# The last MLP of a decoder layer: its up product as seven products of quarter matrices

## The chip, the cores and the metric

The kernel runs on one core of a Trainium2 chip. What counts is the device time of one execution in microseconds (us). Before the change the median of three runs is 1575.95 us (1574.12 to 1577.76). The engines are PE (matrix products; its weight loads are listed apart as PEld), DVE (vector), ACT (scalar and activation), POOL (GpSimd, elementwise work from SBUF only) and SP (it issues most DMA transfers, in order).

## What is computed

One layer of a decoder on 1024 prompt tokens and 32 sample tokens, model width 1024: modulated norm, one input projection, stick-breaking attention in eight heads and a gated recurrence in eight heads, an output projection, and a squared-ReLU MLP. For this change only the MLP matters:

```python
h2 = rms_norm(x, n2) * (1 + sc2) + sh2
x = x + g2 * (jnp.square(jax.nn.relu(h2 @ w_up)) @ w_down)   # w_up (1024, 4096), w_down (4096, 1024)
```

All of it is float32. The kernel writes each factor of a product as a sum of two rounded parts, `hi` and `lo`, and adds three matmuls: hi by hi, hi by lo, lo by hi. Making the two parts (`split`, L147 to L150) is a cast on ACT and a subtraction on DVE or POOL.

## The kernel before

The program is one long list of instructions for each engine, laid down by a scheduler from generators that the source interleaves. In order of time: input projection and recurrence; the first attention; the output projection of prompt tokens 0 to 511; then the first MLP (those 512 tokens) interleaved with the decode of the sample tokens and the second attention (tokens 512 to 1023); the second output projection (`out_projection`, token tiles in the order 4, 5, 8, 6, 7, where 8 is the 32 sample tokens); the last MLP on tokens 512 to 1055, 544 columns in all.

`mlp` (L1171) serves both MLPs. It goes through eight blocks of 512 hidden units. In a block the up product takes four weight pieces of 1024 by 128 (`piece`, loaded in one transfer each into the ring `wraw` of the pool `weights`, split into `whi` and `wlo`), and for each it makes 128 hidden units by all columns: eight contraction steps of three matmuls (L202 to L204). Each result is evicted by ACT (relu L1189, cast L1191) and DVE (square L1190, subtraction L1192) into `uh` and `ul`, which are the moving factors of the down product. The down product adds 8 x 128 output columns into the accumulators `acc` (DVE, L1250). In the last MLP the 544 columns go as a chunk of 256 and one of 288, and weights stand still while columns move. The ring `wraw` has existed since the start of the program, so the scheduler may issue a weight load long before its use.

`modulate` (L307) makes the columns of the last MLP's input from the normalised rows of a tile: transposes on PE (`ptx`, L314), scale and shift on ACT (`hf`, L319) or DVE, the cast `h_hi` (L328) on DVE and the subtraction `h_lo` (L329) on DVE or POOL. The rows of a tile are scaled at L1161 (`xr`), after the sums of squares and a reciprocal root of eleven tiny DVE operations (L134 to L142).

Two generators are interleaved in the middle of the program by weights, the first MLP (`WM` = 64 for its steps) and decode with the second attention (`W[3]` = 166):

```python
x = min(steps, key=lambda x: (x[2] + 0.5) / x[1])   # the one that is least far along goes next
```

The output projection's first weights (`woraw`, L1111), the reads of x (`xres`, L1231) and the stores of the first MLP's results (`out_dram`, L1237) stand in SP's queue in a fixed order and go one after another.

Of the kernel before, what the change touches and what calls it, by code (L numbers as in the profile page):

```python
# [20 lines left out]
P = 128  # L21
D = 1024
# [22 lines left out]
CS = ((256,),(256,))  # L45
# [16 lines left out]
NFX = 8  # L62
# [17 lines left out]
def hymba_step(ctx, tc, x_p, x_s, ck, cv, st_in, ptab, c_p, c_s, w_ada, b_ada, n1g, n2g, w_in,  # L80
# [226 lines left out]
    def modulate(pl, xn, r, c0, a, b, hi_all, lo_all, bufs, kind="r", nu=NU, e=None, ks=(range(4), range(4, 8)), hs=None):  # L307

        for kr in ks:
# [18 lines left out]
            V.tensor_copy(hi_all[:, kk, c0:c0 + r], hf)  # L328
            (e or (G if g and r == P else V)).tensor_tensor(lo_all[:, kk, c0:c0 + r], hf, hi_all[:, kk, c0:c0 + r].bitcast(F32), op=sub)  # L329
# [690 lines left out]
    HW = 544  # L1020
    mmbank = lambda shape, name: bank("mm", shape, name)
# [29 lines left out]
    def out_projection(pl, wpl, tiles, t0, h_hi, h_lo, ks, parts):  # L1051
# [77 lines left out]
        for i, t in enumerate(tiles):  # L1129
# [16 lines left out]
            with tc.high_priority(offset=PN if t in (3, 7) else PN0):  # L1146
# [15 lines left out]
                modulate(pl, xx, r, t * P - t0, a2, b2, h_hi, h_lo, 2)  # L1162
# [6 lines left out]
    def mlp(h_hi, h_lo, t0, chunks, fp, nx, side=iter(())):  # L1169
# [4 lines left out]
        res = {}  # L1174
        if n > 512:
            res_s = fp.tile([NS, D], F32, name="res_s")
            nc.sync.dma_start(res_s, x1d[T:TA, :])
        else:
            g2b = fp.tile([P, D], F32, name="g2b")
        acc = [lp.tile([P, HW], F32, name=f"acc{c}", tag="acc", bufs=8) for c in range(KT)]  # L1180
        for blk in range(NBLK):
            u_hi, u_lo, ws = [], [], []
            cuts = (0,) + CS[t0 > 0] + (n,)
# [24 lines left out]
            if n == 512 and blk == NBLK - 1:  # L1208
                nc.sync.dma_start(g2b, g2d.to_broadcast([P, D]))
            for half_ in range(2) if n == 512 else ():  # L1210
# [29 lines left out]
            for c in range(KT) if n > 512 else ():  # L1240
# [3 lines left out]
                if blk < NBLK - 1:  # L1244
                    def out_y(ci, pm):
                        cs = chunks[ci]
# [4 lines left out]
                    stationary_weights(*w, u_hi, u_lo, NK, chunks, mlpbank, out_y)  # L1251
                else:

                    cc = slice(c * P, (c + 1) * P)
                    g2s = g2[:, c, 1:9].unsqueeze(2).to_broadcast([P, NB, 4])
                    samp = lambda a: a.rearrange("p (b t) -> p b t", t=4)
                    S.activation(acc[c][:, 0:512], acc[c][:, 0:512], AF.Identity, scale=g2[:, c, 0:1])
                    if n > 512:
                        V.tensor_tensor(samp(acc[c][:, 512:n]), samp(acc[c][:, 512:n]), g2s, op=mult)
                    for cs in chunks[::-1]:  # L1260
                        def out_y(_, pm):
                            e = min(cs.stop, 512) - cs.start
                            V.scalar_tensor_tensor(acc[c][:, cs.start:cs.start + e], pm[:, 0:e], g2[:, c, 0:1],
                                                   acc[c][:, cs.start:cs.start + e], op0=mult, op1=add)
                            if cs.stop > 512:
                                ys = fp.tile([P, NS], F32, name="ys", bufs=2)
                                V.tensor_tensor(samp(ys), samp(pm[:, e:e + NS]), g2s, op=mult)
                                V.tensor_tensor(acc[c][:, 512:n], acc[c][:, 512:n], ys, op=add)
                        stationary_weights(*w, u_hi, u_lo, NK, [cs], mlpbank, out_y)
                        with tc.high_priority(offset=PY):  # L1270
                            o, nt = cs.start, (min(cs.stop, 512) - cs.start) // P
                            rows = slice(t0 + o, t0 + o + nt * P)
                            view = lambda a, c0, w: a[rows, P * c0:P * (c0 + w)].rearrange("(u p) c -> p u c", p=P)
                            if c % 2 == 0:
                                res[o] = fp.tile([P, nt, 2 * P], F32, name="xres", tag="xres", bufs=nx)
                                nc.sync.dma_start(res[o], view(x1d, c, 2))
                            xr = res[o][:, :, P * (c % 2):P * (c % 2 + 1)]
                            pt = bank("y", [P, 4, P], "pty")
                            for u in range(nt):
                                TE.transpose(pt[:, u, :], acc[c][:, o + u * P:o + (u + 1) * P], ident)  # L1280
                            if cs.stop > 512:
                                TE.transpose(pt[:NS, nt, :], acc[c][:, 512:n], ident)
                            V.tensor_tensor(xr, pt[:, :nt], xr, op=add)
                            if c >= KT - YS:
                                nc.sync.dma_start(view(y_p, c, 1), xr)
                            elif c % 2 == 1:
                                nc.sync.dma_start(view(y_p, c - 1, 2), res[o])
# [45 lines left out]
    for _ in mlp(*h2, 512, [slice(0, 256), slice(256, 544)], pool("final"), NFX):  # L1333
        pass
# [32 lines left out]
```

## Time and profile before

| | |
|---|---|
| median of 3 runs | 1575.95 us |
| profiled execution | 1573.13 us |
| its span, first to last instruction | 1571.4 us |
| PE busy | 1522.4 us (97%) |
| DVE busy | 980.1 us (62%) |
| ACT busy | 623.9 us (40%) |
| POOL busy | 356.2 us (23%) |
| mean DMA rate | 142 GB/s |
| mean granted TensorE clock | 0.988 of full speed |
| chain of waits that ended last, by engine | PE 81%, DVE 8%, DMA 6% |

Busy shares are means over stages with different limits; a stage is read by the wait that ends last in it. Matmuls are pipelined, so the spacing of their starts, and not the duration of one, is what a matmul costs PE.

### The profile page before, as it was taken

How to read it: one execution, taken by the hardware profiler on the slowest of the kernel's cores; microseconds unless marked ns; L12 is line 12 of the kernel's file. 1: busy time of each engine (PE TensorE's matmuls, PEld its weight loads, DVE VectorE, ACT ScalarE, POOL GpSimd, SP SyncE). 2: the span in 40 equal slices, each digit the busy share in tenths (PEclk: the TensorE clock that was granted, in tenths of full speed). 3: DMA queues.
4: the chain of work that ended last, by engine and by line, in shares of the span. 5: the costliest groups of instructions: out<-in, count | busy, mean ns of one | idle time of the engine just before them, and what ended most of it. 6: DMA issues, size and time to landing. Idle time of an engine off the chain costs nothing.

```text
span 1571.4 us, 26224 instructions
## 1 busy us (share of the span) xinstructions
PE 1522.4 (97%) x9629; PEld 1276.1 (81%) x9629; DVE 980.1 (62%) x2084; ACT 623.9 (40%) x1187; POOL 356.2 (23%) x568
## 2 busy tenths in 40 slices
PE   7999999999999989999998999999899999999998
PEld 3666689998998777765566788888479999999998
DVE  4976438888866862444544977887585344444445
ACT  3742244444423453432232665655345322233330
POOL 0200125544210120000111776793110000000000
PEclk8999999999999989999998999999999999999999
DMA  9389873533124466667465374642744222322221
GB/s 327 110 282 308 259 216 67 111 65 76 50 62 143 135 193 216 204 220 248 150 153 126 98 139 99 137 117 90 234 149 146 87 89 87 94 82 86 89 82 58
DMA packets 249413, 223.14 MB, mean 142 GB/s; under 512 B 60507, under 2 KB 196259, under 8 KB 247236
## 3 DMA queue, kind: packets, MB, share of 16 engines
q1 hardware_dynamic: 186308, 199.26, 40.4%
q0 software_dynamic: 62976, 22.20, 8.4%
q8 instruction: 76, 1.25, 0.3%
q14 instruction: 53, 0.43, 0.1%
HBM read 190.14 MB, written 31.11 MB: 141 GB/s over the span
## 4 chain that ended last, share of the span: by engine, by line
PE 81%; DVE 8%; DMA 6%; issue 2%; ACT 2%; POOL 1%; SPq 0%; POOLq 0%; ACTq 0%; DVEq 0%
PE pm L202 15%; PE pm L203 15%; PE pm L204 15%; PE pm_qkv L215 3%; PE pm L1219 3%; PE pm_qkv L213 3%; PE pm_qkv L214 3%; PE pm L1221 3%; PE pm L1220 3%; PE pod L675 2%; PE ptd L625 2%; DMA wraw<-in_w_up_dram 1%; PE ptw L922 1%; DVE om L909 1%; PE pm_o L1143 1%
## 5 line engine op out<-in xcount | busy, mean ns | idle before, releaser
L202 PE MATMUL pm<-h_hi,whi 128*128 128x288 f32 (+3 forms) x1184 | 384.3, 326 | 4.9 <-DVE gg L792 1.7
L203 PE MATMUL pm<-h_lo,whi 128*128 128x288 f32 (+3 forms) x1184 | 381.9, 323 | 0.3 <-DVE h_lo L329 0.2
L204 PE MATMUL pm<-h_hi,wlo 128*128 128x288 f32 (+3 forms) x1184 | 380.9, 322 | 0.0
L149 ACT CAST whi<-wraw 128x1024 fp32r<-128x1024 f32 x160 | 167.9, 1052 | 317.9 <-PE pm L203 211.5
L150 DVE TENSOR_TENSOR wlo<-wraw,whi 128x1024 fp32r<-128x1024 f32 x144 | 185.1, 1286 | 157.5 <-ACT whi L149 151.6
L202 PEld LDWEIGHTS pm<-h_hi,whi 128*128 128x128 f32 x1184 | 223.6, 189 | 27.0 <-issue 9.8
L204 PEld LDWEIGHTS pm<-h_hi,wlo 128*128 128x128 f32 x1184 | 224.0, 189 | 10.3 <-issue 1.2
L203 PEld LDWEIGHTS pm<-h_lo,whi 128*128 128x128 f32 x1184 | 223.8, 189 | 9.6 <-DVE h_lo L329 0.9
L203 PE MATMUL pm<-ul,whi 128*128 128x256 f32 (+1 forms) x512 | 145.7, 288 | 0.0
L204 PE MATMUL pm<-uh,wlo 128*128 128x256 f32 (+1 forms) x512 | 145.5, 288 | 0.0
L202 PE MATMUL pm<-uh,whi 128*128 128x256 f32 (+1 forms) x512 | 143.7, 289 | 0.0
L909 DVE TENSOR_TENSOR_SCAN om<-om 128x128 f32<-128x128 f32 (+3 forms) x96 | 110.1, 1151 | 27.1 <-POOL om L903 18.8
L150 POOL TENSOR_TENSOR wlo<-wraw,whi 128x1024 fp32r<-128x1024 f32 x16 | 38.5, 2406 | 389.6 <-ACT whi L149 344.1
L910 POOL TENSOR_TENSOR be<-be,om 128x384 f32<-128x384 f32 (+3 forms) x96 | 100.2, 1053 | 51.5 <-DVE om L909 45.2
L1219 PE MATMUL pm<-whi,uh 128*128 128x512 f32 x256 | 106.1, 415 | 2.4 <-DVE acc L1227 2.2
L1221 PE MATMUL pm<-whi,ul 128*128 128x512 f32 x256 | 103.1, 406 | 1.6 <-DVE ul L1192 1.6
L1220 PE MATMUL pm<-wlo,uh 128*128 128x512 f32 x256 | 102.4, 401 | 0.0
L204 PEld LDWEIGHTS pm<-uh,wlo 128*128 128x128 f32 x512 | 95.9, 188 | 0.0
L203 PEld LDWEIGHTS pm<-ul,whi 128*128 128x128 f32 x512 | 95.9, 188 | 0.0
L202 PEld LDWEIGHTS pm<-uh,whi 128*128 128x128 f32 x512 | 94.6, 188 | 0.1
L1250 DVE TENSOR_TENSOR acc<-acc,pm 128x256 f32<-128x256 f32 (+1 forms) x96 | 41.0, 436 | 69.2 <-PE pm L204 69.2
L215 PE MATMUL pm_qkv<-whi,h_lo 128*128 128x512 f32 x192 | 77.6, 405 | 0.8 <-DVE h_lo L329 0.8
(354 smaller groups left out, 2860.9 us busy)
## 6 DMA issues: line engine op xcount, KB each, us to landing
wraw<-in_w_up_dram SPq DMA_DIRECT2D x64, 512.0 KB, 4.0
wraw<-in_w_down_dram SPq DMA_DIRECT2D x64, 512.0 KB, 4.8
wada<-in_w_ada_dram SPq DMA_DIRECT2D x16, 1024.0 KB, 9.1
raw<-in_cache_k_dram SPq DMA_DIRECT2D x64, 256.0 KB, 3.3
vt<-in_cache_v_dram SPq DMA_DIRECT2D x64, 256.0 KB, 3.9
wraw<-in_w_in_dram SPq DMA_DIRECT2D x24, 512.0 KB, 5.7
wa<-in_w_ada_dram SPq DMA_DIRECT2D x16, 512.0 KB, 6.4
qkd<-th SPq DMA_DIRECT2D x16, 256.0 KB, 7.1
```

Source lines behind the costliest of these rows:

```text
L149: (V.tensor_copy if h is V else S.copy)(hi, src)
L150: (e or V).tensor_tensor(lo, src, hi.bitcast(F32), op=sub)
L202: TE.matmul(pm, w_hi[:, k, :], r_hi[k][:, cs], start=(k == 0), stop=False)
L203: TE.matmul(pm, w_hi[:, k, :], r_lo[k][:, cs], start=False, stop=False)
L204: TE.matmul(pm, w_lo[:, k, :], r_hi[k][:, cs], start=False, stop=(k == nk - 1))
L213: TE.matmul(pm, h_hi[:, k, cs], hi, start=(k == 0), stop=False)
L215: TE.matmul(pm, h_lo[:, k, cs], hi, start=False, stop=(k == KT - 1))
L909: V.tensor_tensor_scan(back, back, back, 1.0 if right is None else right[:, 0:1], op0=mult, op1=ALU.bypass)
L910: G.tensor_tensor(be[:, 0:w], be[:, 0:w], om[:, 1:w + 1], op=mult)
L1219: TE.matmul(pm, u_hi[m][:, ts], hi, start=(m == 0), stop=False)
L1220: TE.matmul(pm, u_hi[m][:, ts], lo, start=False, stop=False)
L1221: TE.matmul(pm, u_lo[m][:, ts], hi, start=False, stop=(m == NK - 1))
```

## The change

The last MLP leaves `mlp` and gets a function of its own, `last_mlp`. `mlp` keeps the first 512 tokens only; its last `yield` moves out of the down loop, so that the first MLP has one more step in each block (70 steps in all, where there were 62).

The 544 columns become two halves of 272: tiles 4 and 5 with 16 sample tokens, tiles 6 and 7 with the other 16. Two neighbouring blocks of 128 hidden units form a *unit*; its weights are a 2 x 2 array of quarters (two column blocks by two halves of the contraction), and the tokens' input is one too (two halves of the contraction by two halves of the columns). The product of the two arrays is made by Winograd's form of Strassen's method with seven quarter products (`p1` to `p7`) in place of eight. Each quarter product is four contraction steps of three matmuls by 272 columns. The sums of token quarters are made once, ahead of block 0; those of weight quarters for each unit, on POOL (L1288 to L1291), and all sums are split into hi and lo anew. Quarter products are added up in part in the accumulation of matmuls and in part by DVE.

The weights of a unit are loaded into `uraw` (two pieces, two buffers each), which lies in the pool `final`; that pool is opened where the output projection's pool `outp1` has been closed, in the same memory. The weights of the down product go through the old ring.

```diff
-    def mlp(h_hi, h_lo, t0, chunks, fp, nx, side=iter(())):
+    def mlp(h_hi, h_lo, chunks, fp, nx, side=iter(())):
...
                     if tt % 2:
                         yield
-            for c in range(KT) if n > 512 else ():
+            yield
+
+    def last_mlp(h_hi, h_lo, fp):
...
+        tok = [slice(0, HH), slice(HH, HW)]
+        k1, k2 = range(4), range(4, 8)
...
+        for q in range(2):
+            b = {}
+            for i, (kq, c) in enumerate(((0, 0), (0, 1), (4, 1), (4, 0))):
+                kk = slice(kq + 2 * q, kq + 2 * q + 2)
+                x = lp.tile([P, 2, HH], F32, name="bq", tag="u", bufs=8)
+                (G if i > 1 else V).tensor_tensor(x, h_hi[:, kk, tok[c]].bitcast(F32), h_lo[:, kk, tok[c]].bitcast(F32), op=add)
+                b[kq // 4, c] = x
+            kk = slice(2 * q, 2 * q + 2)
+            V.tensor_tensor(b[0, 0], b[0, 1], b[0, 0], op=sub)
+            G.tensor_tensor(b[0, 1], b[1, 1], b[0, 1], op=sub)
+            V.tensor_tensor(b[1, 1], b[1, 1], b[0, 0], op=sub)
+            G.tensor_tensor(b[1, 0], b[1, 0], b[1, 1], op=sub)
+            for hi, lo, x, e in ((t_hi[:, 0, kk], t_lo[:, 0, kk], b[1, 1], V), (t_hi[:, 1, kk], t_lo[:, 1, kk], b[0, 1], V),
+                                 (h_hi[:, kk, tok[1]], h_lo[:, kk, tok[1]], b[0, 0], G), (t_hi[:, 2, kk], t_lo[:, 2, kk], b[1, 0], V)):
+                split(hi, lo, x, e)
...
+        def unit_weights(c0):
+
+            with tc.high_priority(offset=PW):
+                raw = [fp.tile([P, KT, P], F32, name="uraw", bufs=2) for _ in range(2)]
+                for i in range(2):
+                    nc.sync.dma_start(raw[i], wview(w_up, 0, KT, c0 + P * i, P))
...
+                split(whi, wlo, raw[0])
+                (a11, a12), (a21, a22) = ((x[:, 0:4], x[:, 4:8]) for x in raw)
+                s = [fp.tile([P, 4, P], F32, name="sx", tag="xres", bufs=NFX) for _ in range(4)]
+                G.tensor_tensor(s[0], a21, a22, op=add)
+                G.tensor_tensor(s[1], s[0], a11, op=sub)
+                G.tensor_tensor(s[2], a11, a21, op=sub)
+                G.tensor_tensor(s[3], a12, s[1], op=sub)
+                parts = {}
+                for name, x in (("p6", s[1]), ("p7", s[2]), ("p5", s[0]), ("p4", a22), ("p3", s[3])):
+                    hi = fp.tile([P, 4, P], F32R, name="shi", bufs=NSW)
+                    lo = fp.tile([P, 4, P], F32R, name="slo", bufs=NSW)
+                    split(hi, lo, x)
+                    parts[name] = (hi, lo)
+            parts.update(p1=(whi[:, 0:4], wlo[:, 0:4]), p2=(whi[:, 4:8], wlo[:, 4:8]))
+            return parts
...
+            for i, w in enumerate(units):
+                b, c, e, x2 = upbank(), upbank(), upbank(), q2[i]
+                x3 = quarter("q3", 2)
+                multiply(b, w, "p6", True)
+                with tc.high_priority(offset=PV):
+                    V.tensor_tensor(x2, b, x2, op=add)
+                multiply(c, w, "p7", True)
...
+                    V.tensor_tensor(x3, c, x2, op=add)
+                multiply(e, w, "p5", True)
...
+                    V.tensor_tensor(x3, e, x3, op=add)
+                    done(2 * i + 1, 1, x3, 1)
+                multiply(c, w, "p4", False)
...
+                multiply(e, w, "p3", False)
...
-    for _ in mlp(*h2, 512, [slice(0, 256), slice(256, 544)], pool("final"), NFX):
-        pass
+    rstack.close()
+    last_mlp(*h2, pool("final"))
```

(`V` is DVE, `S` ACT, `G` POOL; `wview` is a view of a weight in memory; `done` makes the relu, the square and the two parts `uh` and `ul` of one quarter of the result.)

The scheduler lays the instructions down anew. Three places matter below.

**From the first MLP to the second output projection, SP.** The rows are transfers: `out_dram` is a store of the first MLP's result, `xres` a read of x for it, `woraw` the output projection's first two weights. Before:

```order
L1237 DMA out_dram<-xres 128x512
L1231 DMA xres<-x1d 128x512 x2
L1237 DMA out_dram<-xres 128x512 x2
L936 DMA mixa_63<-tv 64x256
L1231 DMA xres<-x1d 128x512 x2
L1111 DMA woraw<-in_w_out_dram 128x1024 x2
L1066 DMA mr<-mixa_62 128x4x128
```

With the change:

```order
L1240 DMA out_dram<-xres 128x512
L1133 DMA g1s<-g1d 32x1x512
L1116 DMA woraw<-in_w_out_dram 128x1024 x2
L1240 DMA out_dram<-xres 128x512
L1234 DMA xres<-x1d 128x512
L1071 DMA mr<-mixa_62 128x4x128
```

The two weights moved ahead of the last reads and stores of the first MLP. On PE, 48 matmuls of the first MLP (512 columns each) now stand behind the second attention's last product, where 19 stood.

**The start of the last MLP, SP and POOL.** `x1d` is the store of a tile's rows, `uraw` and `wraw` are weights. Of SP before:

```order
L1066 DMA mr<-mixb_65 128x4x128
L1111 DMA woraw<-in_w_out_dram 128x1024
L159 DMA wraw<-in_w_up_dram 128x8x128
L1066 DMA mr<-mixa_63 128x4x128
L1066 DMA mr<-mixb_66 128x4x128
L159 DMA wraw<-in_w_up_dram 128x8x128 x2
L1157 DMA x1d<-xr 128x512
```

Of SP with the change (the next weights of the up product at all):

```order
L1090 DMA xr<-in_x_prompt_dram 128x1024
L1162 DMA x1d<-xr 32x512
L1162 DMA x1d<-xr 128x512 x4
L1282 DMA uraw<-in_w_up_dram 128x8x128 x2
L1250 DMA res_s<-x1d 32x1024
L1282 DMA uraw<-in_w_up_dram 128x8x128 x2
```

The first weights of the up product stood between the transfers of the second tile; now they stand behind the last store of the last tile, and the first of them waits for the scaling of tile 7 (DVE) and for its last transposes (PE), whose memory it takes. POOL with the change, from the last piece of tile 7 on (`bq` are sums of token quarters, `sx` sums of weight quarters, each named with its number); before, the next row of POOL there was the split of a weight piece:

```order
L333 TENSOR_TENSOR h2_lo_12842<-hf_13450,h2_hi_12841 128x4x128
L1263 TENSOR_TENSOR bq_13478<-h2_hi_12841,h2_lo_12842 128x544
L1263 TENSOR_TENSOR bq_13480<-h2_hi_12841,h2_lo_12842 128x544
L151 TENSOR_TENSOR h2_lo_12842<-bq_13474,h2_hi_12841 128x2x272
L1263 TENSOR_TENSOR bq_13498<-h2_hi_12841,h2_lo_12842 128x544
L1263 TENSOR_TENSOR bq_13500<-h2_hi_12841,h2_lo_12842 128x544
L1267 TENSOR_TENSOR bq_13476<-bq_13478,bq_13476 128x544
L151 TENSOR_TENSOR h2_lo_12842<-bq_13494,h2_hi_12841 128x2x272
L1288 TENSOR_TENSOR sx_13522<-uraw_13515 128x512
L1267 TENSOR_TENSOR bq_13496<-bq_13498,bq_13496 128x544
L1269 TENSOR_TENSOR bq_13480<-bq_13480,bq_13478 128x544
L1289 TENSOR_TENSOR sx_13523<-sx_13522,uraw_13514 128x512
```

The weight sum that the product `p6` of the first unit needs (the last row) stands twelfth in this queue; POOL had nothing of the kind before.

**The end of the up product of a block in the middle, DVE.** The numbers are those of block 3; `slo` is the lo part of a weight sum of the next block's first unit, `ul` the lo part of the up product. Before:

```order
L1190 TENSOR_TENSOR rr_15230<-rr_15230 128x288
L1190 TENSOR_TENSOR rr_15268<-rr_15268 128x256
L1192 TENSOR_TENSOR ul2_15174<-rr_15230,uh2_15173 128x288
L1192 TENSOR_TENSOR ul3_15242<-rr_15268,uh3_15241 128x256
L150 TENSOR_TENSOR wlo_15554<-wraw_15551,whi_15553 128x1024
L1190 TENSOR_TENSOR rr_15298<-rr_15298 128x288
```

With the change:

```order
L1321 TENSOR_TENSOR ul3_15261<-rr_15451,uh3_15257 128x272
L151 TENSOR_TENSOR slo_15755<-sx_15747,shi_15754 128x512
L1351 TENSOR_TENSOR q4_15467<-pm_u_15409,q2_15290 128x272
L151 TENSOR_TENSOR slo_15759<-sx_15748,shi_15758 128x512
L1319 SCALAR_TENSOR_TENSOR rr_15469<-q4_15467 128x272
L151 TENSOR_TENSOR slo_15763<-sx_15746,shi_15762 128x512
L151 TENSOR_TENSOR slo_15767<-uraw_15739,shi_15766 128x512
L1355 TENSOR_TENSOR q2_15290<-pm_u_15410,q2_15290 128x272
L151 TENSOR_TENSOR slo_15771<-sx_15749,shi_15770 128x512
L1321 TENSOR_TENSOR ul3_15261<-rr_15469,uh3_15257 128x272
L1319 SCALAR_TENSOR_TENSOR rr_15486<-q2_15290 128x272
L1321 TENSOR_TENSOR ul2_15260<-rr_15486,uh2_15256 128x272
```

Five splits for the next block stand among this block's last evictions. The last of them (`slo_15771`) needs the fourth weight sum from POOL, and the last two parts `ul` of this block stand behind it. The second raw piece `uraw_15739` of that next unit is issued by SP only when DVE has split its predecessor, in the middle of the up product.

## Rows read from the trace of the kernel before

**Rows 1.** The page's head: span, and busy time of each engine.

```profile
span 1571.4 us, 26224 instructions
...
PE 1522.4 (97%) x9629; PEld 1276.1 (81%) x9629; DVE 980.1 (62%) x2084; ACT 623.9 (40%) x1187; POOL 356.2 (23%) x568
```

**Rows 2.** Timeline of PE (start, duration): block 1 begins, its down half, block 7.

```profile
1225.22 0.28 PE L202 MATMUL pm<-h_hi,whi 128*128 128x256 f32 x1
...
1249.32 0.28 PE L202 MATMUL pm<-uh,whi 128*128 128x256 f32 x1
...
1514.04 0.28 PE L202 MATMUL pm<-h_hi,whi 128*128 128x256 f32 x1
```

**Rows 3.** A block: window, us, busy PE, PEld, DVE, ACT, POOL, clock, DMA share, GB/s.

```profile
1346.80:1394.90 48.10, 48.10 (x386) 48.10 (x385) 21.58 (x39) 14.16 (x25) 2.39 (x1) 1.00 0.29 89
```

**Rows 4.** Timeline of PE where the second output projection begins.

```profile
1112.95 1.06 PE L1097 MATMUL pm_os<-woraw,smp_k 128*32 128x512 f32 x1 [6.39 <-DMA woraw<-in_w_out_dram]
...
1116.95 0.59 PE L1097 MATMUL pm_os<-woraw,smp_k 128*32 128x512 f32 x1
```

**Rows 5.** Timeline of SP's queue, ahead of that.

```profile
1106.85 1.44 SPq L1231 DMA_DIRECT2D xres<-x1d  x2
1108.34 0.90 SPq L1111 DMA_DIRECT2D woraw<-in_w_out_dram  x2
```

**Rows 6.** Timeline of PE, second attention's first product and matmuls after it.

```profile
832.07 0.44 PE L895 MATMUL pz<-kk,qh 128*128 128x128 f32 x1 [5.05 <-DMA kk<-qkd]
...
835.96 0.63 PE L1219 MATMUL pm<-whi,uh 128*128 128x512 f32 x1
```

**Rows 7.** Timelines: PE's last output-projection matmul, tile 7's scaling on DVE, its transposes.

```profile
1173.19 0.39 PE L1145 MATMUL pm_o<-wo,ml 128*128 128x512 f32 x1
...
1184.76 0.88 DVE L1161 TENSOR_SCALAR xr<-xr,s 128x512 f32<-128x512 f32 x2
...
1186.22 1.03 PE L314 MATMUL ptx<-ident,xr 128*128 128x128 f32 x8
```

**Rows 8.** The page's DMA issues: count, KB each, us from issue to landing.

```profile
wraw<-in_w_up_dram SPq DMA_DIRECT2D x64, 512.0 KB, 4.0
```

**Rows 9.** Groups by form, 1100 to 1571.4 us: busy us, mean ns, idle before.

```profile
L149 ACT CAST whi<-wraw 128x1024 fp32r<-128x1024 f32 x65 | 68.3, 1051 | 171.1 <-PE pm L203 153.9 <-DMA wraw<-in_w_out_dram 5.2 <-DMA wraw<-in_w_up_dram 4.8
...
L150 DVE TENSOR_TENSOR wlo<-wraw,whi 128x1024 fp32r<-128x1024 f32 x57 | 69.8, 1225 | 99.8 <-ACT whi L149 99.4
L1250 DVE TENSOR_TENSOR acc<-acc,pm 128x288 f32<-128x288 f32 x48 | 21.2, 453 | 44.4 <-PE pm L204 44.4
...
L329 DVE TENSOR_TENSOR h_lo<-hf,h_hi 128x512 fp32r<-128x512 f32 x4 | 2.7, 679 | 0.0
```

**Rows 10.** Timelines of POOL and DVE at two splits on POOL.

```profile
1156.37 1.29 POOL L329 TENSOR_TENSOR h_lo<-hf,h_hi 128x512 fp32r<-128x512 f32 x1 [43.97 <-DVE rs_t L140]
...
1156.74 0.68 DVE L225 TENSOR_TENSOR tp<-tp,pm_os 32x512 f32<-32x512 f32 x1 [0.25 <-ACT tp L223]
...
1182.63 1.47 POOL L329 TENSOR_TENSOR h_lo<-hf,h_hi 128x512 fp32r<-128x512 f32 x1 [7.74 <-DVE s L142]
...
1181.77 0.15 DVE L139 TENSOR_TENSOR rs_t<-s 128x1 f32<-128x1 f32 x1
...
1182.87 1.25 DVE L139 TENSOR_TENSOR rs_t<-s 128x1 f32<-128x1 f32 x1
```

**Rows 11.** Timelines of POOL and DVE in the second attention.

```profile
1002.11 1.09 POOL L910 TENSOR_TENSOR be<-be,om 128x512 f32<-128x512 f32 x1 [1.25 <-DVE om L909]
1003.15 0.29 POOL L903 TENSOR_SCALAR_AFFINE_SELECT om<-om 128x128 f32<-128x128 f32 x1
...
1007.47 0.82 POOL L903 TENSOR_SCALAR_AFFINE_SELECT om<-om 128x128 f32<-128x128 f32 x1 [1.87 <-ACT om L899]
...
1007.47 0.67 DVE L1192 TENSOR_TENSOR ul<-rr,uh 128x512 fp32r<-128x512 f32 x1
```

**Rows 12.** The second attention by windows, columns as in rows 3.

```profile
1000.00:1040.00 40.00, 40.00 (x217) 33.91 (x216) 33.65 (x40) 24.99 (x47) 30.74 (x43) 1.00 0.52 124
```

More of the change, by code (lines that the diff above doesn't have):

```diff
@@ L44 @@
 RE = 0
-CS = ((256,),(256,))
+CS = (256,)
 BF = dict(m="012345", y="67")
@@ L61 @@
 NPR = 2
-NFX = 8
+NFX = 4
+NSW = 5
 PQ0 = 100
@@ L327, in modulate @@
                     V.tensor_copy(hs[:, kk], hf)
-            V.tensor_copy(hi_all[:, kk, c0:c0 + r], hf)
-            (e or (G if g and r == P else V)).tensor_tensor(lo_all[:, kk, c0:c0 + r], hf, hi_all[:, kk, c0:c0 + r].bitcast(F32), op=sub)
+            hi, lo = (at(x[:, kk]) if at else x[:, kk, c0:c0 + r] for x in (hi_all, lo_all))
+            if at:
+                hf = hf.rearrange("p k (g x) -> p k g x", g=2)
+            V.tensor_copy(hi, hf)
+            (e or (G if g and r == P else V)).tensor_tensor(lo, hf, hi.bitcast(F32), op=sub)
     with ExitStack() as s0:
@@ L1161, in out_projection @@
                     V.tensor_scalar(x, x, s2[:, 0:1], None, op0=mult)
-                modulate(pl, xx, r, t * P - t0, a2, b2, h_hi, h_lo, 2)
+                half = lambda a: a.rearrange("p k (g x) -> p k g x", x=HH)[:, :, :, 256:HH]
+                c0 = t * P - t0 + (HH - 256) * (not early and t > 5)
+                modulate(pl, xx, r, c0, a2, b2, h_hi, h_lo, 2, at=half if t == NT else None)
     FB_ = 512
@@ L1207, in mlp @@
                     yield
-            if n == 512 and blk == NBLK - 1:
+            if blk == NBLK - 1:
                 nc.sync.dma_start(g2b, g2d.to_broadcast([P, D]))
-            for half_ in range(2) if n == 512 else ():
+            for half_ in range(2):
                 cc = slice(512 * half_, 512 * (half_ + 1))
@@ L1250, in out_y @@
                             V.tensor_tensor(acc[c][:, cs], acc[c][:, cs], pm, op=add)
[L1251 to L1287, printed above, removed]
-                            if cs.stop > 512:
-                                V.tensor_tensor(res_s[:, cc], pt[:NS, nt], res_s[:, cc], op=add)
-                                if c % 4 == 3:
-                                    cc4 = slice((c - 3) * P, (c + 1) * P)
-                                    nc.sync.dma_start(y_s[:, cc4], res_s[:, cc4])
@@ L1293, in mlp @@
-                yield
+                    stationary_weights(*w, u_hi, u_lo, NK, tok, mlpbank, out_y)
+                    continue
+                cc = slice(c * P, (c + 1) * P)
+                prompt = by_half(acc[c])[:, :, 0:256]
+                S.activation(prompt, prompt, AF.Identity, scale=g2[:, c, 0:1])
+                samp = lambda a: a.rearrange("p (b t) -> p b t", t=4)
+                g2s = g2[:, c, 1:9].unsqueeze(2).to_broadcast([P, NB, 4])
+                sa = fp.tile([P, NS], F32, name="sa", bufs=2)
```

108 lines of the change are left out of this document (96 added, 12 removed).

## The prediction

> **What bounds the kernel now.** I read the page's head first, then the windows of the last MLP, then the places where PE stood still, and last what DVE and POOL do to each other. PE is busy 1522.4 us of a span of 1571.4 [rows 1], so time is won by giving PE less to do or by closing its gaps, and lost by opening new ones. In the last MLP PE has no gap at all: 48.10 us of matmuls in a window of 48.10, at full clock, while DVE works 21.58 us, ACT 14.16 and POOL 2.39 [rows 3]. Blocks follow each other every 48.14 us (1225.22 to 1514.04 is six of them), and the up half takes 24.10 us of one [rows 2]. It is 192 matmuls, half of 256 and half of 288 columns, so one of 272 columns costs 24.10 / 192 = 0.1255 us.
>
> Two gaps stand earlier. Ahead of the second output projection PE waits 6.39 us for `woraw`, and the first matmuls after it take 1.06 us where later ones take 0.59 [rows 4]: half the pace, the lower of the clock's two levels. SP reached that load at 1108.34, behind reads and stores of the first MLP [rows 5]. And before the second attention's first product PE waits 5.05 us for `kk`, and the matmuls after that last 0.63 us, at the lower clock again [rows 6].
>
> **The saving.** A unit's seven products are 84 matmuls of 272 columns instead of 96; a block's up product is 168 x 0.1255 = 21.09 us instead of 24.10. That is 3.01 us a block and **24.1 us** in all if PE stays dense. The down product costs the same.
>
> **The start of the last MLP.** Before, weights lay ready, and PE passed from the last matmul of the output projection (1173.19) straight to the up product, working on the columns of earlier tiles while tile 7 was still being scaled (1184.76 to 1185.64) and transposed [rows 7]. Now the first weight waits for that scaling. I put its issue at 1185.3 (the first evictions no longer stand in DVE's queue), its landing 4.0 + 0.4 us later [rows 8] at 1189.7, and with the cast (1.05 us) and two older casts ahead of it on ACT the first matmul at 1193: PE does nothing but transposes for 20 us. `p1` and `p2` of the first unit, at the lower clock at first, last to 1198. `p6` needs the twelfth row of POOL's new queue. POOL starts on it at 1189.0; three of the twelve are 512 columns (1.29 us, [rows 10]) and nine are 544 (1.37, by columns): 16.2 us, so 1205.2, and with cast and split `p6` starts at 1206.5. The second unit's weights wait for the fourth sum: issue 1209.2, landing 1213.6, its products end about 1228, and 192 down matmuls (24.1 us) end block 0 at 1252. Before it ended at 1225.22 [rows 2]. So the start costs **27 us** if each engine goes at its own pace, already net of that block's saving.
>
> It will not. Rows 10 show why. The operation `rs_t` is 128 x 1 and takes 0.15 us at 1181.77; at 1182.87, just after POOL had begun a split (1182.63, 1.47 us), it takes 1.25 us and ends at 1184.12, two hundredths after POOL does. At 1156.74 a DVE operation that reads one factor from PSUM runs 0.68 us undisturbed beside such a split. The other way round, a POOL operation of 0.29 us takes 0.82 when a DVE subtraction of 0.67 has started at the same instant [rows 11]. So POOL and a DVE operation with both inputs in SBUF exclude each other for the whole of an instruction. The Trainium skill states it as a rule (SBUF — State Buffer, section "Who interferes with whom"): the port pair of the two engines is an exclusive lock, held for a whole instruction, and a DVE instruction with both inputs in SBUF contends with a GpSimd instruction that reads SBUF, while one with at most one such input and no two-port mode does not. By that rule the sum is the one I take; without it, rival B.
>
> Between 1189 and `p6` DVE has 11 such operations of 544 columns (0.679 x 544 / 512 = 0.72 us, [rows 9]), a split of 1.23, one of 0.68 and two of about 0.45, all told 10.7 us, and POOL 16.2. One after another that is 27 us, plus one or two POOL operations that slip in between. `p6` then starts about 1217, 11 us later, and all behind it too. Bounds for the whole start: 23 (POOL at the 1.09 us that an operation of 512 columns took at 1002.11 [rows 11], 0.2 less for each of 19 operations, and no exclusion) and 44. I take **+38**, since the rows show exclusion wherever the two meet.
>
> **Blocks 1 to 7.** PE gives 3.01 us back in each unless something stalls it; seven make 21.1. DVE goes from 21.58 us a block [rows 3] to about 33 of 45: in a unit five splits of 512 (0.68) and one of 1024 (1.23), four evictions of three or four operations (0.45), POOL to eight sums (10.3). Over the block there is room; at the end of the up product there is none. Walking DVE's order of block 3 with these durations, from its first matmul on, DVE has split the fourth part of the running set at 15.0 us; only then is the next unit's second raw piece issued; it lands at 19.4; POOL's four sums take 5.2 us, to 24.6; the last split, two `ul` and a square behind it bring the last `ul` at 27.8. PE wants it at 28.2. That is a margin of 0.4 us with no exclusion. With it, the four sums and 6 us of DVE's operations go in turn: the last sum at 26.3, the last `ul` at 31.9, a stall of 3.7 us. Bounds 0 and 3.7 us a block. I take 2.5, nearer to the upper one by rows 10, because the additions from PSUM can run beside POOL. So each block gains 0.5 us: **-3.5**.
>
> **The first MLP's new step.** `woraw` stands ahead of the last reads and stores in SP's queue, and 48 matmuls of 512 columns stand behind the second attention, 29 more than before, nearly 7 us of cover. The wait of 6.39 shrinks to about 1.5, and the slow matmuls after it lose their cause (six pairs at twice the time, 1.7 us): **-6.5**, bounds -8.5 (all of it) and 0 (the second attention, where DVE is busy 33.65 of 40 us and POOL 30.74 [rows 12], is late by what it gave away). The wait of 5.05 us for `kk` has about five more matmuls of cover; I count it with this term. The tail has one more transpose pair: +0.5.
>
> **Sum.** The profiled execution took 1573.13 us, 2.8 below the median. 1573.1 - 6.5 + 38 - 3.5 + 0.5 = 1601.6; with 2.8 for the median **1604 us**, 1.8% slower. What this can tell from no change is 0.2%, 3.15 us.
>
> **Rivals.**
> *A, the forecast*: chance 0.62, 1604; its own range 1592 to 1618.
> *B, the engines rarely meet (faster).* If the sums on POOL fall into times when DVE adds from PSUM or waits, nothing is held: the start costs 23 and every block gains its 3.0. 1573.1 - 6.5 + 23 - 21.1 + 0.5 + 2.8 = 1572, 0.25% faster. It decides at a hold of under 0.4 us in the up half of a block. For it: DVE has 12 us to spare over a block. Against it: rows 10 and 11, and the queue at the end of the up product, where sums and splits fall together by their order. Chance 0.17, half of it beyond the bound of 0.2%.
> *C, both early gaps close.* If the second attention's first product is reached with its keys landed, 5.05 us and 2.5 us of half clock [rows 6] come off too: 1604 - 7.5 = 1596. Chance 0.10.
> *D, no gain ahead of the last MLP.* The second attention leans on DVE and POOL for most of its time [rows 12]; with fewer matmuls beside it, its waits show. Then the 6.5 us don't come, and with the full 3.7 us in every block it is 1604 + 6.5 + 8.4 = 1619. Chance 0.11.
> *The change doesn't save matmuls*: excluded, since the order has 360 of 272 columns in a block.
>
> **Numbers.** Low 1574 leaves out the better part of B, high 1619 takes in nearly all of D; about 0.8 lies between. Faster: half of B and a little, 0.12. Same: the other half, 0.08. Slower: A, C, D, 0.80.
>
> **What would show it.** In the profile after: PE without matmuls from about 1167 for 20 us (the early gain moves all by 6), then a second gap of 15 to 20 before `p6`, with the granted clock down in that stretch; POOL's sums or DVE's splits at 1.5 to 2.2 us instead of 1.3 and 0.7; blocks of 47 to 48 us, with PE waiting for DVE `ul` or ACT `uh` once in each. Block 0 ending over 33 us later than 1225.22 less the early gain bears out the start; blocks of 45.1 us with splits at 0.7 would prove the exclusion wrong and give B; a wait for `woraw` still at 6 would prove the early term wrong.

## The result, and the profile after

| | before | after |
|---|---|---|
| median of the runs, us | 1575.03 (1572.32 to 1577.76, 4 runs) | 1613.73 (1611.4 to 1614.78, 4 runs) |
| ratio, 95% interval | | 1.0244 [1.0222, 1.0265] |
| span of the profiled execution, us | 1571.4 | 1611.8 |

The change makes the kernel 2.4% slower; 1604 was forecast, and 1613.73 lies in the range, nearer to the 1619 of rival D than to the forecast. The page's head of the kernel after, beside [rows 1]: PE is busy 5 us less, POOL 101 us more.

```profile
span 1611.8 us, 26201 instructions
...
PE 1517.3 (94%) x9437; PEld 1263.2 (78%) x9437; DVE 1097.9 (68%) x2258; ACT 649.1 (40%) x1227; POOL 457.4 (28%) x634
```

The timeline of PE (start, duration, in brackets the idle time before and what ended it): the end of the second output projection, the first product of the last MLP, `p6` of the first unit and its first `slo`, and where blocks 1, 2, 3 and 7 begin.

```profile
1185.03 0.40 PE L1150 MATMUL pm_o<-wo,ml 128*128 128x512 f32 x1
...
1205.98 0.60 PE L1304 MATMUL pm_u<-h_hi,whi 128*128 128x272 f32 x1 [10.58 <-ACT whi L150]
...
1221.70 0.60 PE L1304 MATMUL pm_u<-t_hi,shi 128*128 128x272 f32 x1 [7.19 <-ACT shi L150]
...
1225.17 0.60 PE L1306 MATMUL pm_u<-t_hi,slo 128*128 128x272 f32 x1 [2.65 <-DVE slo L151]
...
1279.76 0.29 PE L1304 MATMUL pm_u<-h_hi,whi 128*128 128x272 f32 x1
...
1326.00 0.29 PE L1304 MATMUL pm_u<-h_hi,whi 128*128 128x272 f32 x1
...
1372.06 0.29 PE L1304 MATMUL pm_u<-h_hi,whi 128*128 128x272 f32 x1
...
1556.17 0.29 PE L1304 MATMUL pm_u<-h_hi,whi 128*128 128x272 f32 x1
```

Set beside [rows 2, 7], these rows split the 40.4 us by which the two profiled executions differ (the medians differ by 38.7). The last matmul of the projection moves from 1173.19 to 1185.03: **+11.8**, all of it ahead of the last MLP. From there to the end of block 0 it was 52.03 us and is 94.73: the start costs **+42.7**. Blocks 1 to 6 take 276.41 us instead of 288.82, 46.07 each instead of 48.14: **-12.4**. From block 7's first matmul to the end it is 55.63 instead of 57.36: **-1.7**. 11.8 + 42.7 - 12.4 - 1.7 = 40.4.

The windows of the start and of block 2 (columns as in [rows 3]):

```profile
1200.00:1220.00 20.00, 6.55 (x24) 5.58 (x24) 15.76 (x10) 5.30 (x9) 19.92 (x13) 0.50 0.05 14
1326.00:1372.06 46.06, 45.79 (x362) 45.37 (x361) 32.42 (x58) 16.66 (x28) 12.89 (x8) 1.00 0.30 92
```

In the start PE has work for a third of the time, at a granted clock of half speed (1.2 GHz), while POOL never rests. In a block PE is again all but full; DVE has 32.42 us of work where it had 21.58.

### The profile page after: what moved, and what is told of

It reads as the page before. It is cut to its first block, busy times and chain, and to the rows that moved or that the text cites. A ratio compares the mean times of both kernels' runs of the same rounds, so it can differ in the third digit from the quotient of the medians.

```text
span 1611.8 us, 26201 instructions
## 1 busy us (share of the span) xinstructions
PE 1517.3 (94%) x9437; PEld 1263.2 (78%) x9437; DVE 1097.9 (68%) x2258; ACT 649.1 (40%) x1227; POOL 457.4 (28%) x634
## 4 chain that ended last, share of the span: by engine, by line
PE 72%; DVE 11%; DMA 8%; issue 4%; POOL 3%; ACT 2%; SPq 1%; POOLq 0%; ACTq 0%; DVEq 0%
PE pm L204 9%; PE pm L203 9%; PE pm L205 9%; PE pm L1222 3%; PE pm L1223 3%; PE pm L1224 3%; PE pm_qkv L216 3%; PE pm_qkv L214 3%; PE pm_qkv L215 3%; PE pm_u L1304 2%; PE pm_u L1305 2%; PE pm_u L1306 2%; DMA kk<-qkd 2%; PE ptd L629 2%; PE pod L679 2%
## 5 line engine op out<-in xcount | busy, mean ns | idle before, releaser
L203 PE MATMUL pm<-h_hi,whi 128*128 128x384 f32 (+3 forms) x672 | 236.4, 353 | 4.7 <-DVE gg L796 1.7
L204 PE MATMUL pm<-h_lo,whi 128*128 128x384 f32 (+3 forms) x672 | 235.1, 350 | 0.1
L205 PE MATMUL pm<-h_hi,wlo 128*128 128x384 f32 (+3 forms) x672 | 235.1, 350 | 0.0
L204 PE MATMUL pm<-ul,whi 128*128 128x272 f32 x512 | 146.6, 291 | 0.6 <-DVE ul L1321 0.6
L203 PEld LDWEIGHTS pm<-h_hi,whi 128*128 128x128 f32 x672 | 127.7, 190 | 22.0 <-issue 4.4
L203 PE MATMUL pm<-uh,whi 128*128 128x272 f32 x512 | 140.6, 291 | 4.5 <-DVE q L1355 4.0
L205 PE MATMUL pm<-uh,wlo 128*128 128x272 f32 x512 | 144.3, 288 | 0.0
L204 PEld LDWEIGHTS pm<-h_lo,whi 128*128 128x128 f32 x672 | 128.0, 191 | 12.0 <-issue 2.5
L205 PEld LDWEIGHTS pm<-h_hi,wlo 128*128 128x128 f32 x672 | 127.8, 190 | 11.9 <-issue 2.9
L914 POOL TENSOR_TENSOR be<-be,om 128x128 f32<-128x128 f32 (+3 forms) x96 | 99.5, 1046 | 29.1 <-DVE om L913 22.1
L1288 POOL TENSOR_TENSOR sx<-uraw 128x512 f32<-128x512 f32 x16 | 22.2, 1387 | 228.0 <-DVE q L1343 105.6
```

Of the source, the lines that this page charges most:

```text
L203: TE.matmul(pm, w_hi[:, k, :], r_hi[k][:, cs], start=(k == 0), stop=False)
L204: TE.matmul(pm, w_hi[:, k, :], r_lo[k][:, cs], start=False, stop=False)
L205: TE.matmul(pm, w_lo[:, k, :], r_hi[k][:, cs], start=False, stop=(k == nk - 1))
L914: G.tensor_tensor(be[:, 0:w], be[:, 0:w], om[:, 1:w + 1], op=mult)
```

## The experiments

Spans are compared with 1611.8 (after) and 1571.4 (before), single runs unless an interval stands beside them. In the traces of the ten kernels below without the moved step the last matmul of the projection (last `pm_o`) comes anywhere from 1173.9 to 1181.8 us, though their sources differ only in the last MLP. So places in the last MLP are given from it, and a difference of a few us between two single spans shows nothing by itself.

**The moved `yield`.** What does it give ahead of the last MLP? `yield_back` takes it out of the kernel after, at the end of a block of `mlp` (all later runs but `yield_alone` build on this one), and `yield_alone` puts it alone into the kernel before, in the same place:

```diff
-            yield
```

```diff
+            if n == 512:
+                yield
```

> The changed kernel with the first MLP's extra step taken out again (62 steps, as before the change); the last MLP is untouched. Theory: the extra step alone let decode and attention run ahead of the first MLP and cost the 11.8 us by which the last matmul of the second output projection came late (1185.0 instead of 1173.2). Then that matmul comes at 1173 to 1175, block 0 of the last MLP takes as long as in the changed kernel, and the span is 1599 to 1602. Rival: the lateness comes from the closed pool or the smaller tiles; then it stays at 1185 and the span at 1611.

> The kernel before with nothing but the extra step of the first MLP added. Theory: the last matmul of the second output projection comes at 1183 to 1187 instead of 1173.2, and the span grows by as much, to 1581 to 1586. Rival (the step is harmless): 1571 to 1573.

`yield_back`: 1604.17 us, ratio to before 1.019 [1.0166, 1.0214], span 1602.2; the last `pm_o` comes at 1176.74 and block 0 ends 94.0 after it, about as in the kernel after (94.7). The median is 9.6 us below that of the kernel after. `yield_alone`: span 1579.3, the last `pm_o` at 1181.03, 7.8 later than in the trace of before, and 2 us earlier than I expected; its one execution took 1580.97, 4.7 above the median of 13 executions of before that were measured with it and 2.4 above the slowest of them. So the moved step costs some 5 to 10 us, where I had forecast a gain. PE's waits in `yield_alone` (us in total, times, longest):

```profile
PE pz L895 <- DMA kk<-qkd: 8.2, 2, 7.0
...
PE pm_o L1143 <- ACT mh L149: 3.2, 1, 3.2
```

Its timeline of PE where the second output projection begins, as in [rows 4], and its window that answers to [rows 12]:

```profile
1115.63 0.62 PE L1097 MATMUL pm_os<-woraw,smp_k 128*32 128x512 f32 x1
```
```profile
1000.00:1040.00 40.00, 36.05 (x185) 30.06 (x184) 25.10 (x34) 20.42 (x40) 22.20 (x33) 0.96 0.48 97
```

The wait of 6.39 us for `woraw` ahead of the projection [rows 4] is gone, as forecast, and nothing is won by it. PE reaches the second attention earlier and waits 7.0 us for `kk` instead of 5.05 [rows 6]; between 1000 and 1040 it now idles 4 us where it was full; it begins the projection at 1115.63 instead of 1112.95 in spite of the wait it lost, and then waits 3.2 us for `mh`, the split of the mix, which before was got ready while PE stood waiting for `woraw`. In `yield_back` the first two are as they were: 4.9 us for `kk`, and PE full between 1000 and 1040. These waits are not the whole of the 7.8 us: up to the last `pm_o` PE stands idle for 48.7 us instead of 44.4, and the other 3.6 are time in matmuls, not traced further.

**The start: the sums of the tokens.** `tokens_dve` is `yield_back` with all sums and splits of `h` on DVE:

```diff
-                (G if i > 1 else V).tensor_tensor(x, ...
+                V.tensor_tensor(x, ...
...
-            G.tensor_tensor(b[0, 1], b[1, 1], b[0, 1], op=sub)
+            V.tensor_tensor(b[0, 1], b[1, 1], b[0, 1], op=sub)
...
-            G.tensor_tensor(b[1, 0], b[1, 0], b[1, 1], op=sub)
+            V.tensor_tensor(b[1, 0], b[1, 0], b[1, 1], op=sub)
...
-                                 (h_hi[:, kk, tok[1]], h_lo[:, kk, tok[1]], b[0, 0], G), ...
+                                 (h_hi[:, kk, tok[1]], h_lo[:, kk, tok[1]], b[0, 0], V), ...
```

> As yield_back, with all sums and splits of token quarters on DVE; POOL keeps the sums of weight quarters alone. Theory (DVE with both inputs in SBUF and POOL exclude each other, so the two queues ahead of the product p6 add up): nine operations of 1.37 us on POOL become nine of 0.72 on DVE, and p6 of the first unit starts 5 to 8 us earlier against the last output-projection matmul than the 36.7 us of the changed kernel; the whole is 5 to 8 us faster than yield_back. Rival (each engine at its own pace): DVE's queue becomes 17 us, no shorter than POOL's 16, and nothing is gained, 0 to 2 us.

Span 1592.9, 9.3 below `yield_back`: `p6` starts 29.02 after the last `pm_o` instead of 36.81, and block 0 ends 83.4 after it instead of 94.0. DVE alone does this work sooner than the two together: 7.8 us at `p6`, within the theory's 5 to 8 and beyond the rival's 0 to 2. These rows of the kernel after say why, first POOL's timeline, then DVE's:

```profile
1200.26 3.46 POOL L1263 TENSOR_TENSOR bq<-h_hi,h_lo 128x544 f32<-128x544 f32 x2
1203.68 1.81 POOL L151 TENSOR_TENSOR h_lo<-bq,h_hi 128x544 fp32r<-128x544 f32 x1
```
```profile
1197.36 0.72 DVE L1263 TENSOR_TENSOR bq<-h_hi,h_lo 128x544 f32<-128x544 f32 x1
...
1198.97 3.56 DVE L1263 TENSOR_TENSOR bq<-h_hi,h_lo 128x544 f32<-128x544 f32 x2
1202.56 1.73 DVE L1266 TENSOR_TENSOR bq<-bq 128x544 f32<-128x544 f32 x1
```

A sum of 544 columns takes DVE 0.72 us at 1197.36; once POOL is at work, two take 3.56 on DVE and two take 3.46 on POOL. While both run, an operation of either takes about 1.75 us, not far from one of DVE and one of POOL together (0.72, and 1.33 for POOL's quickest here).

**The start: the first unit's raw pieces.** `first_unit_ring` is `yield_back` with the first unit's pieces in the ring of the other weights, so that they load ahead of the scaling of tile 7:

```diff
-                raw = [fp.tile([P, KT, P], F32, name="uraw", bufs=2) for _ in range(2)]
+                raw = [wp.tile([P, KT, P], F32, name="wraw", tag="wraw", bufs=NWR) if c0 == 0 else fp.tile([P, KT, P], F32, name="uraw", bufs=2) for _ in range(2)]
```

> As yield_back, with the first unit's weights loaded into the old ring, where they can land during the output projection. Theory: the loss ahead of p6 is the queue of sums on POOL and DVE, not the wait for the weights. Then p1 starts within 4 us of the last output-projection matmul instead of 21.1, but p6 starts 33 to 38 us after it, as in yield_back (36.8); block 0 gains 4 to 9 us all the same, since the second unit no longer waits for the first one's buffers. Rival (the weights are what is late): p6 starts 10 us earlier or more, and the whole is over 10 us faster than yield_back.

`p1` starts 2.7 after the last `pm_o` instead of 21.1, and `p6` 36.84, as before: 18 us of wait in one place buy 3.7 at the end of block 0 (90.4 instead of 94.0), a little less than expected. The span of 1603.9 is above that of `yield_back` all the same, since the last `pm_o` comes 5.1 later (1181.79). The first gap was not what set the end of the start. The queue of sums ahead of `p6` was: `tokens_dve` and the next run each shorten it, and `p6` comes 7 to 8 us earlier; and behind `p6` PE here waits three times, 6.3 us in all, for `t_lo`, the lo part of a sum of the tokens.

**The weight sums.** `no_weight_sums` is `yield_back` with quarters in place of the sums, so it leaves the sums out:

```diff
-                s = [fp.tile([P, 4, P], F32, name="sx", tag="xres", bufs=NFX) for _ in range(4)]
...
+                s = [a22, a11, a21, a12]
```

> As yield_back, with the four sums of weight quarters of each unit left out (a quarter itself is split and multiplied in place of each sum, so the up product is not the reference's); POOL has nothing to do in blocks 1 to 7. Theory: the 0.9 us by which a block of 46.05 exceeds 360 matmuls of 0.1255 us comes from the chain raw piece, four sums, split, last ul; then blocks take 45.1 to 45.4 us, and ahead of block 0 the product p6, freed of two sums in POOL's queue, starts 3 to 6 us earlier than 36.8 us after the last output-projection matmul. Rival (the amount of DVE's work alone): blocks stay at 45.9 to 46.1.

Blocks 2 to 6 take 45.15 to 45.18 us, which is 360 x 0.1255: PE is dense. `p6` comes at 29.62 instead of 36.81, and the span is 1584.7. So the 0.9 us by which blocks of the kernel after stand above that belong to the weight sums, and so do 7 us of the way to `p6` and 11.5 of that to the end of block 0 (82.5 instead of 94.0). This run takes away both the sums' own time and their meeting with DVE's operations; it does not say which of the two counts.

**An ordinary first block.** `plain_first` is `yield_back` with block 0's up product of four whole pieces, in halves of 272 tokens, while the tokens' sums are made behind it (their temporaries in the ring of `sx`); `plain_256` cuts the tokens at 256 (`for cs in (slice(0, 256), slice(256, HW))`); `plain_256_dve` also has the tokens' sums on DVE. Core of the edit:

```diff
+        ws = [piece([wview(w_up, 0, KT, m * P, P)], KT, P, V) for m in range(NK)]
+        for cs in tok:
+            for m in range(NK):
...
+                stationary_weights(*ws[m], [h_hi[:, k] for k in range(KT)], [h_lo[:, k] for k in range(KT)], KT, [cs], mlpbank, out_u)
...
+            if blk == 0:
+                u_hi, u_lo = u0
```

> As yield_back, but block 0 makes its up product in the old way, with eight quarter products from the old ring, and the sums of token quarters are made beside it; blocks 1 to 7 use seven products. Theory: the loss of the change lies wholly in what must be ready ahead of block 0. Then block 0 takes 52 to 54 us after the last output-projection matmul, as before (52.0), seven blocks gain 2.1 us each, and the span is 1555 to 1561, faster than both kernels. Rival (the sums are too much work wherever they stand): the first block of seven products stalls by over 8 us, and the span is 1566 or more.

> As plain_first, but the first chunk of block 0's up product is the 256 columns of tiles 4 and 5, without the 16 sample tokens. Theory: in plain_first PE waited 5.2 us at the start of block 0 for the sample tokens' columns; here the up product starts within 0.5 us of the last output-projection matmul and the span is 3 to 6 us under plain_first's 1572.5. Rival: what is won at the start is lost to the sums a few us later, and the span stays within 1.5 us.

> As plain_256, with the sums and splits of token quarters on DVE alone. Theory (exclusion): the evictions of block 0 no longer stand behind POOL's 1.4 us operations, and block 0 takes 52 to 55 us instead of the 60.4 of plain_first, so that the span is 1558 to 1563, 0.8 to 1.1% faster than the kernel before. Rival (DVE has too much to do in block 0, where 17 us are added to 22): block 0 takes 58 us or more and the span is over 1566.

`plain_first`: 1574.34, ratio 0.999 [0.9978, 1.0001], span 1572.5. The first gap shrinks to 5.2, but block 0 ends 65.6 after the last `pm_o`, where I had expected 52 to 54. The rival is not borne out either: the span is above 1566, but the first block of seven products takes 46.0 and does not stall. POOL's and then DVE's timeline in its block 0 show the reason, and the list of PE's waits in that stretch what it costs:

```profile
1206.72 6.10 POOL L1273 TENSOR_TENSOR bq<-h_hi,h_lo 128x544 f32<-128x544 f32 x1 [3.77 <-DVE t_lo L151]
```
```profile
1206.56 1.21 DVE L151 TENSOR_TENSOR wlo<-wraw,whi 128x1024 fp32r<-128x1024 f32 x1
...
1208.68 0.43 DVE L1264 TENSOR_TENSOR ul<-rr,uh 128x272 fp32r<-128x272 f32 x1
...
1218.41 1.57 DVE L1264 TENSOR_TENSOR ul<-rr,uh 128x272 fp32r<-128x272 f32 x1
```
```profile
PE pm L204 <- DVE ul L1264: 5.4, 2, 4.6
```

A sum on POOL is held for 6.10 us while DVE runs one operation after the other undisturbed; then POOL's queue comes late, and holds the `ul` that PE waits for (1.57 us instead of 0.43). `plain_256`: the up product starts 0.2 after the last `pm_o`, and block 0 ends 63.2 after it, so half of the 5.0 us won is lost again behind; the other half doesn't show in the span (1572.6), since the last `pm_o` itself comes 2.5 later than in `plain_first`. With the sums on DVE, `plain_256_dve` takes **1569.67 us, ratio 0.9959 [0.9945, 0.9973]** (span 1564.2, of the second fastest of six executions; four of them are above 1566): block 0 ends 58.0 after the last `pm_o`, blocks 3 to 6 take 46.02. That is 5 us less than with POOL, but not the 52 to 55 expected: 58 was the rival's, that DVE has much to do there.

**The last 0.9 us of a block.** `three_raw` is `plain_256_dve` with a third buffer for the raw pieces (the two pieces of a unit share two buffers in all, not two each as the part on the change has it), and `sums_dve` is `three_raw` with the weights' sums on DVE:

```diff
-                raw = [fp.tile([P, KT, P], F32, name="uraw", bufs=2) for _ in range(2)]
+                raw = [fp.tile([P, KT, P], F32, name="uraw", bufs=3) for _ in range(2)]
```

```diff
-                G.tensor_tensor(s[0], a21, a22, op=add)
+                V.tensor_tensor(s[0], a21, a22, op=add)
...
-                G.tensor_tensor(s[3], a12, s[1], op=sub)
+                V.tensor_tensor(s[3], a12, s[1], op=sub)
```

> The same as plain_256_dve, with three buffers for the raw pieces of a unit of w_up instead of two, so that the second piece of the next unit is issued without waiting for the fourth split. Theory: the last 0.9 us by which a block stands above 45.15 is the chain raw piece, sums, split, ul; the sums then start 2 to 4 us earlier, blocks take 45.1 to 45.5 instead of 46.02, block 0 ends 1 to 3 us earlier relative to the last pm_o, and the span is 1556 to 1561 instead of 1564.2. Rival (the sums wait for their buffers or for DVE, not for the raw piece): blocks stay at 45.9 to 46.1 and the span at 1564 within 2.

> three_raw with the four sums of a unit of w_up on DVE instead of POOL. Theory: POOL is idle in a block and nothing is held; DVE has about 6 us more a block and still 8 to spare, so blocks take 45.1 to 45.8, and block 0 ends within 2 us of three_raw's; span within 3 of three_raw's. Rival (DVE's queue, not the hold between POOL and DVE, is what is short at the end of the up product): blocks above 46.3, span 3 to 12 above three_raw's.

`three_raw` went the other way from what I expected, and further than the rival: 1576.23 us, ratio 1.0006 [0.9994, 1.0018], blocks 2 to 6 at 47.2 to 47.7. The pieces do come earlier, and the sums on POOL with them (the first at 6.1 us into block 3 instead of 18.4), but now they run while DVE does the squares of the up product. The groups by form of the six blocks from block 2 on hold 36 squares, 0.43 us each when nothing holds them: first in `plain_256_dve`, then in `three_raw`, then in `sums_dve`:

```profile
L1329 DVE SCALAR_TENSOR_TENSOR rr<-q 128x272 f32<-128x272 f32 x36 | 17.7, 492 | 0.4
```
```profile
L1329 DVE SCALAR_TENSOR_TENSOR rr<-q 128x272 f32<-128x272 f32 x36 | 33.6, 935 | 0.4
```
```profile
L1329 DVE SCALAR_TENSOR_TENSOR rr<-q 128x272 f32<-128x272 f32 x36 | 15.6, 434 | 0.1
```

In `sums_dve` nothing is held: a sum takes DVE 0.68 us, a square 0.43, and the window of block 3 shows PE full with POOL idle.

```profile
1326.52:1371.67 45.15, 45.15 (x362) 45.15 (x361) 33.97 (x66) 16.62 (x28) 0.00 (x0) 1.00 0.31 94
```

It takes **1564.06 us, ratio 0.9936 [0.9919, 0.9952]**, the best of the study: blocks 1 to 6 at 45.15 to 45.17. The rival (DVE's queue too full) is refuted: DVE's 33.97 us of 45.15 cost nothing. The span lies 12 us below that of `three_raw`, not within 3 as I expected. Against before (1562.5 for 1571.4) blocks 1 to 6 give 17.9 and the rest behind them 2.0; 6.1 are lost in block 0, 4.9 of them as PE's waits (1.8 for `ul`, 1.7 for `h_hi`, 1.4 for `rr`), and 4.9 ahead of the last `pm_o`, whose cause was not sought.

**What is left of the start without POOL.** `all_dve` is `tokens_dve` with the weights' sums on DVE, so the change as it stands without any work on POOL in the last MLP:

> tokens_dve with the four sums of a unit of w_up on DVE as well: the change as it stands (all blocks with seven products, the yield back in its place), with POOL out of the last MLP. Theory (what is left of the start is the chain from the scaling of tile 7 through the first unit's weights, not the hold between DVE and POOL): blocks 1 to 7 at 45.15, block 0 ends 80 to 85 after the last pm_o, as in tokens_dve (83.4), and the span is 1583 to 1590, slower than before. Rival (what is left of the start is the hold): block 0 ends under 75 after the last pm_o and the span is under 1577.

Span 1584.9; blocks 1 to 6 at 45.12 to 45.38; block 0 ends 80.3 after the last `pm_o`. So with the sums on DVE two raw buffers do as well as three, within 0.3 us a block: the 0.9 us were POOL's part (its longer operation and the hold, which no run takes apart) and not the late raw piece by itself. PE's timeline:

```profile
1193.32 0.59 PE L1303 MATMUL pm_u<-h_hi,whi 128*128 128x272 f32 x1 [5.33 <-ACT whi L150]
...
1199.79 0.60 PE L1305 MATMUL pm_u<-h_hi,wlo 128*128 128x272 f32 x1 [5.66 <-DVE wlo L151]
```

Of the 42.7 us that the start costs, about 14 are POOL's part, the hold and its longer operations (94.0 to 80.3), and 28 remain. I put them down to the chain from tile 7's scaling through the first unit's weights, with DVE's queue in it, since PE's longest waits there (the two above, and 7.3 at tile 7's transposes) lie on it; no run takes that chain away while POOL is idle. An ordinary first block takes most of these away (58.1 in `sums_dve`).

## Why the prediction was right, and which of its steps were not

The verdict and the mechanism were right: the start costs more than dense blocks give back, and POOL's new work is held by DVE's and holds it. The sizes:

| term of the sum | forecast (bounds) | measured |
|---|---|---|
| ahead of the last MLP | -6.5 (-8.5 to 0) | +11.8 |
| start, to the end of block 0 | +38 (23 to 44) | +42.7 |
| blocks 1 to 7 and the tail | -3.5 + 0.5 | -14.1 |
| sum, profiled execution | +28.5 | +40.4 |

**The step that failed is "The first MLP's new step".** I put the `woraw` wait down as idle time that 29 more matmuls would fill. They were taken from the second attention, which needed them: `kk` is reached earlier and waited for longer, new idle time opens between 1000 and 1040, and the projection, reached without the wait, finds its other input, `mh`, late. The sign I had named, a wait for `woraw` still at 6, could not show this: the wait went, and the term was wrong all the same. Rival D named the reason but allowed for a gain of 0, not a loss, and my upper bound of 0 shut it out. PE's timeline in the kernel after:

```profile
1116.84 0.62 PE L1102 MATMUL pm_os<-woraw,smp_k 128*32 128x512 f32 x1
...
1121.92 0.79 PE L1148 MATMUL pm_o<-wo_hi,mh 128*128 128x512 f32 x1 [4.02 <-ACT mh L150]
...
1171.61 0.50 PE L1148 MATMUL pm_o<-wo_hi,mh 128*128 128x512 f32 x1 [2.73 <-DVE tp L1155]
```

Of the 11.8, the projection begins 3.9 later (1116.84 for 1112.95) and takes 7.9 longer (68.2 us to its last `pm_o` instead of 60.2). Undoing the `yield` gives 9.6 of span back. The last of the three rows does not go back to the `yield`: `yield_back` has the same wait for `tp` (longest 2.7; before and in `yield_alone` 0.7 and 0.6), and its last `pm_o` is still 3.5 late. PE's waits in its projection:

```profile
PE pm_os L1102 <- DMA woraw<-in_w_out_dram: 8.5, 2, 8.2
PE pm_o L1148 <- DVE tp L1155: 3.0, 2, 2.7
```

The longer `woraw` wait (8.2, at another landing time) gives 1.8, the one for `tp` about 2; why either grew was not tried, and the spread of the last `pm_o` among the runs is larger than both.

**The start** was right in its mechanism: 21.0 us from the last `pm_o` to `p1` (forecast 19.8), half clock, POOL's sums at 1.7 us and more. `p6` came 36.7 after the last `pm_o`, where 43.8 was forecast, but from it to the end of block 0 it took 58.1 where 45.5 was: behind `p6` PE waited seven times for DVE (2.65 for `slo`, 2.96 for `q`, the others under 2; 9.6 in all), which my sum priced at nothing. The way to `p6` was priced too high: from POOL's first sum (1200.26) to the end of the one for `p6` (1218.67) it is 18.4 us, not the 27 of all operations one after another. The two errors, 7.1 us over and 12.6 under, cancel in part; that the term comes within 4.7 us is partly luck. The upper bound of 44 had no working.

**Blocks 1 to 7** were mis-sized: a stall of 0.9 us, not 2.5. The first sum of block 2 and the last `ul`, with a sum and a split between them (POOL's timeline, then DVE's):

```profile
1344.28 1.41 POOL L1288 TENSOR_TENSOR sx<-uraw 128x512 f32<-128x512 f32 x1 [26.45 <-DVE q L1343]
...
1348.55 1.75 POOL L1291 TENSOR_TENSOR sx<-uraw,sx 128x512 f32<-128x512 f32 x1
```
```profile
1349.06 0.43 DVE L1351 TENSOR_TENSOR q<-pm_u,q 128x272 f32<-128x272 f32 x1
1349.41 1.44 DVE L151 TENSOR_TENSOR slo<-sx,shi 128x512 fp32r<-128x512 f32 x1
...
1354.55 0.44 DVE L1321 TENSOR_TENSOR ul<-rr,uh 128x272 fp32r<-128x272 f32 x1 [0.48 <-ACT uh L1320]
```

The four sums take 6.0 us (1344.28 to 1350.30), where 5.2 was the time without and 6.9 with the hold; the first began at 18.3 us into the block, not 19.4; the last `ul` ends at 29.0, between the 27.8 and the 31.9 of the two walks. PE's own wait in the block is for an addition `q` that stands in the same queue, behind a split of a weight sum (DVE, then PE):

```profile
1352.33 0.43 DVE L1355 TENSOR_TENSOR q<-pm_u,q 128x272 f32<-128x272 f32 x1
```
```profile
1352.81 0.39 PE L203 MATMUL pm<-uh,whi 128*128 128x272 f32 x1 [0.27 <-DVE q L1355]
```

The rest of the 0.9 shows as wider spacing of the matmuls right at and behind this one, not as idle time. I took a value nearer to the upper bound; the measured one is nearer to the lower, since here only four of DVE's operations ran into a sum, and the additions from PSUM (0.43 at 1349.06, while POOL works) did not.

Two errors of opposite sign, 18.3 us ahead of the last MLP and 11 in its blocks, so made the forecast, 9.7 us short, look better than its steps: that the sum came so near is partly luck. (The 2.8 us that I added for the median did not come back: the profiled execution of the kernel after took 1613.65, its median 1613.73.)

## What to carry to other kernels

A wait of PE that other matmuls are moved into (a filler) is won only if the filler has no use where it was taken from, and if the next input is not late as well: look at what else the waiting stage reads, and let the bound of such a term include a loss. When work is handed to POOL to spare DVE, count what both do with operands in SBUF at the same time: here DVE, 75% busy, did all of it in less time than the two together. A method that saves matmuls in the steady state need not be used in the first block, where the sums it needs have nothing to hide behind: with the first MLP's step as before, an ordinary first block, no sums on POOL and a third raw buffer, the same seven products made the kernel 0.64% faster instead of 2.4% slower.

## What the hardware showed

The hold between DVE and POOL reaches far: a POOL operation of 544 columns, 1.33 us at its quickest in the start of the kernel after, was held for 6.10 in `plain_first`, while DVE's own operations ran at their full pace; in the start of the kernel after the two alternate, and each of DVE's takes 1.7 to 1.9 us instead of 0.72. What decides between the two cases was not tried. The Trainium skill's rule (SBUF — State Buffer, section "Who interferes with whom") has the lock exclusive and held for an instruction; both cases agree with that, and with it that the additions from PSUM were not held (0.43 us beside a sum on POOL).

And loading earlier can be slower: one more buffer for the raw pieces moved the sums beside the squares, and blocks went from 46.02 us to between 47.2 and 47.7.
